# The first norm of a two-layer encoder: row scales as a diagonal in the transposes, the weight behind them, constants loaded later

## The chip, the core and the metric

The kernel runs on one core of a Trainium2 chip. The metric is the device time of one execution in microseconds (us). TensorE (PE) multiplies matrices, and loads their stationary operands (PEld) beside that; VectorE (DVE) and ScalarE (ACT) do elementwise work, GpSimd (POOL) a few small operations. DMAs are issued from SyncE's queue (SP) and from ACT's.

## The reference

One sequence of 256 tokens, width 1024, runs through two layers of: a SwiGLU, four mixers side by side, a second SwiGLU, each between two RMS norms. All is float32. What the change touches is the very first norm and the start of the first SwiGLU:

```python
def rms_norm(x, g):
    y = xf * lax.rsqrt(jnp.mean(xf * xf, axis=-1, keepdims=True) + RMS_EPS)
    return (y * g).astype(x.dtype)

def swiglu(h, w_gate, w_up, w_down):
    return (silu(h @ w_gate) * (h @ w_up)) @ w_down
...
    h = rms_norm(x, g[0])
    x = x + 0.5 * rms_norm(swiglu(h, w_gate, w_up, w_down), g[1])
```

## The kernel before

The 256 tokens are two row tiles (tk 0 and 1) of 128. Products keep float32 precision by splitting both operands into a rounded part and a remainder, hi and lo, and adding three products (`TERMS`): hi*hi, hi*lo, lo*hi. Weights come from HBM in chunks of 128x1024 (512 KB, `f_raw`, four buffers), one DMA each on SP's queue (`Stream.next`, L243); ACT makes `f_hi` and DVE `f_lo`. The first four chunks are split in halves of 512 columns (`SPLITC`). A chunk's DMA waits until the DVE remainder of the chunk four places ahead has released the buffer.

The norm is `norm_t` (L284 and on), for one row tile: ACT squares the two halves of x and sums (`jk`), DVE adds the sums (`st`), POOL takes the power -0.5 (`r_n`), DVE multiplies x by the norm's weight (`xg`, with `gain`, the weight broadcast to all 128 rows: 512 KB), DVE and ACT scale half of `xg` each by the row scale (L297 and the line behind). Then `turn` transposes `xg` in eight 128x128 pieces on TensorE (`pt`, L310) into two PSUM tiles of four pieces, and ACT and DVE split them into the hi and lo of `XT`, 256 columns at a time (L315). `XT` holds the transposed, normed input: `XT_00` to `XT_03` have two of the eight pieces k each, for both row tiles.

The first SwiGLU starts before all is there. `half_block(0, 0)` (`pgh`, L395) multiplies row tile 0 with the first block's gate and up weights (chunks f0 for k 0 to 3 and f1 for k 4 to 7) as soon as its norm is done; then the second norm's `turn` runs, then row tile 1 of the same block (`half_block(0, 1)`). From block 1 on (`block`: `pg`, L418 and L419, chunks f2 and f3; then f4 and f5) both row tiles go together. `rows` (L438) is the down product `y`, with a chunk of its own for each block: f6 is the first. In the program names end in a number; in the order of the kernel before, f0, f1, f2 and f3 are `f_raw_144`, `152`, `222` and `230`, f4 to f6 are `238`, `244` and `250`, and their split parts have slightly higher numbers.

Instructions are written in the order of the functions, and a scheduling layer then places them in each engine's queue and adds the semaphores; eight semaphores serve the DMAs in turn, so that a DMA also waits for one some places ahead. `WARM` products of zeros keep TensorE busy before x arrives. `load_small(l)` loads the constants `C`, the decay logits `lg` and the parameters `par`; `held` places its instructions behind those in `mid`, which are ACT's and DVE's last of an early block of the first SwiGLU; with no DMA among them, the DMAs of `load_small(0)` stand near the start of SP's queue.

Of the kernel before, what the change touches and what calls it, by code (L numbers as in the profile page):

```python
# [9 lines left out]
F32 = mybir.dt.float32  # L10
F32R = mybir.dt.float32r
BF16 = mybir.dt.bfloat16
# [5 lines left out]
P = 128  # L18
# [87 lines left out]
def tile_encoder(ctx: ExitStack, tc: tile.TileContext, x_in, wffn, win, wout, gains, params, idn, cst, rel, out, dbg=None):  # L106
# [31 lines left out]
    def stt(out, a, s, b, op0, op1):  # L138
        V.scalar_tensor_tensor(out=out, in0=a, scalar=s, in1=b, op0=op0, op1=op1)  # L139

    def act(out, a, f, **kw):
        return A.activation(out, a, f, **kw)  # L142
# [4 lines left out]
    def f(a):  # L147
        return a.bitcast(F32)
# [13 lines left out]
    def s1(name, shape=(P, S), dt=F32):  # L162
        return sp.tile(list(shape), dt, tag="s1", bufs=4, name=name)
# [63 lines left out]
    @contextmanager  # L227
    def held(*ins):

        with ExitStack() as c:  # L230
            for i in ins:
                c.enter_context(tc.issue_after(i.ins))
            yield

    class Stream:
# [4 lines left out]

        def next(self, pool=None):
            r = rawp.tile([P, 1024], F32, tag="raw", name=f"{self.name}raw{self.i}")
            nc.sync.dma_start(out=r, in_=self.dram[:, self.i * 1024:(self.i + 1) * 1024])  # L243
            if self.first and self.i == 1:
                load_x(1, 0)
                load_x(1, 1)
            new = pool or (w4, w4)
            hi = new[0]([P, 1024], F32R, name=f"{self.name}hi{self.i}")
            lo = new[1]([P, 1024], F32R, name=f"{self.name}lo{self.i}")
            n = 2 if self.i < SPLITC else 1  # L250
            with held(*self.hold.get(self.i, ())):
                for c in range(n):
                    cs = slice(c * 1024 // n, (c + 1) * 1024 // n)
                    act(hi[:, cs], r[:, cs], AF.Copy)
                    sub(lo[:, cs], r[:, cs], f(hi[:, cs]))
            self.i += 1
            return hi, lo
# [3 lines left out]
    def gain(l, i):  # L261
        t = k4([P, D], name=f"gain{l}_{i}")
        nc.scalar.dma_start(out=t, in_=gains[l, i:i + 1, :].broadcast_to([P, D]))
        return t

    def rstd(ms, n, name):
        r = sp.tile([P, 8], F32, tag="rstd", bufs=4, name=name)
        tt(r[:, 0:n], ms, nhalf[:, 0:n], ALU.pow, G)
        return r
# [9 lines left out]
    def xt2(XT, k):  # L279

        return XT[k // 2][:, k % 2, :, :]

    def norm_t(XT, g, tk, tag, hold=()):

# [70 lines left out]


    TA, TB, TC, SG = 4, 2, 5, 2
    NPRO, NEPI, SPLITC, WARM, W_FIN, ZW = 3, 7, 4, 8, 4.0, 2
    RATIO, RATIO2, W_PREP, W_INV, GRAIN, R1, R2, WQ, QG, KD = 0.8, 0.6, 4, 12, 0.8, 1.4, 2.2, 0.12, 8, 2

    def ffn(hold, l, j, XT, before2, ahead, after, first, last, mix_next):
# [126 lines left out]
        for fb in range(fb0, NFB - 3):  # L488
            fetch_ab(fb + 1)
            fetch_d(fb + 1)  # L490
            early = block(fb + 1)
            if fb == fb0 + 3:
                mid = early
            rows([fb], 0)
            if fb < NFB - NEPI:
                rows([fb], 1)
# [808 lines left out]
    gi = {("f", 0): 0, ("m", 0): 2, ("f", 1): 4}  # L1305
    XT = new_xt(0, 0)
    load_x(0, 0)
    g0 = gain(0, 0)
    load_x(0, 1)
    nc.sync.dma_start(out=ident, in_=idn)  # L1310
    act(warm, ones1, AF.Silu)

    pq = ps.tile([P, 256], F32, tag="o", bufs=1, name="pq")
    z = SB[0][0].rearrange("p a b c -> p (a b c)")
    for i in range(WARM):
        T.matmul(pq, lhsT=z[:, 0:P], rhs=z, start=True, stop=True)
    done = norm_t(XT, g0, 0, "d")()
    pend = lambda: norm_t(XT0, g0, 1, "a", done[1])
    XT0, done = XT, {0: done[0], 1: done[1]}
    for n, (kind, l, j) in enumerate(seq):  # L1320
        i = gi[(kind, j)]
# [118 lines left out]
```

## Time and profile before

| | |
|---|---|
| time, median of 3 runs | 1170.97 us (1168.13 to 1174.04) |
| profiled execution | 1175.67 us, of which the span of instructions 1174.0 us |
| granted TensorE clock, mean | 0.984 |
| busy: PE / PEld / DVE / ACT / POOL | 97 / 82 / 68 / 55 / 8% of the span |
| read from HBM | 187.62 MB, 161 GB/s over the span |

The page gives busy times of each engine over the whole span; the part that the change touches is its first 26 us, for which the timeline (each instruction's start and length, and in brackets the idle time before it and what ended it) and the waits are read. L121, L139 and L142 are helpers that issue most elementwise work of DVE and ACT, so those instructions are told apart by their tiles.

### The profile page before, as it was taken

To read this page: it belongs to the slowest core of one execution; us is meant where nothing else is said; L and a number is where in the kernel's file an instruction comes from. 1 tells how busy PE (TensorE), PEld (TensorE's weight loads), DVE (VectorE), ACT (ScalarE), POOL (GpSimd) and SP (SyncE) were. 2 spreads that over 40 slices of the span, in tenths; PEclk is the share of its full clock that TensorE was granted. 3 is DMA by queue.
4 is the path that set the end of the run, shared out by engine and by line. 5 is a ranking of instruction groups with operands and counts; after the bars stand their busy time and mean duration, and the time that the engine had idled before them with its cause. 6 is when DMAs were issued, how large, how long until landed. Compare 5 with 4: busy or idle time off the path is not lost. (4 is left out here: it accounts for less than half of the span.)

```text
span 1174.0 us, 20406 instructions
## 1 busy us (share of the span) xinstructions
PE 1133.7 (97%) x8084; PEld 966.0 (82%) x8084; DVE 799.9 (68%) x1351; ACT 641.9 (55%) x1159; POOL 92.3 (8%) x159
## 2 busy tenths in 40 slices
PE   7999999979999999999999999999799999999997
PEld 6888888877888888887788888889778888888886
DVE  6656566797775866665676666667896669565663
ACT  6565555757333655554655555557473357455562
POOL 0000000243100000000000000013431000000000
PEclk9999999987999999999999999999899999999999
DMA  7755574412341665656546656725124326565650
GB/s 276 238 181 189 188 237 140 156 33 82 101 133 58 220 215 182 195 181 211 186 128 210 197 180 196 231 94 180 50 72 145 110 82 207 196 189 188 190 187 36
DMA packets 53088, 189.99 MB, mean 162 GB/s; under 512 B 6144, under 2 KB 6272, under 8 KB 52992
## 3 DMA queue, kind: packets, MB, share of 16 engines
q1 hardware_dynamic: 50976, 181.61, 47.6%
q10 hardware_dynamic: 2016, 7.08, 1.7%
q8 instruction: 63, 1.03, 0.4%
q14 instruction: 33, 0.27, 0.1%
HBM read 187.62 MB, written 1.05 MB: 161 GB/s over the span
## 5 line engine op out<-in xcount | busy, mean ns | idle before, releaser
L121 DVE TENSOR_TENSOR f_lo<-f_raw,f_hi 128x1024 fp32r<-128x1024 f32 (+1 forms) x280 | 323.7, 1162 | 201.1 <-ACT f_hi L142 200.2
L418 PE MATMUL pg<-XT,f_hi 128*128 128x512 f32 x1248 | 444.4, 398 | 3.5 <-DVE gu L121 3.4
L142 ACT ACTIVATE f_hi<-f_raw 128x1024 fp32r<-128x1024 f32 (+1 forms) x280 | 280.1, 1008 | 138.2 <-DMA f_raw<-in_wffn_dram 95.1
L419 PE MATMUL pg<-XT,f_lo 128*128 128x256 f32 x1248 | 350.0, 280 | 0.0
L418 PEld LDWEIGHTS pg<-XT,f_hi 128*128 128x128 f32 x1248 | 234.4, 188 | 62.7 <-DVE gu L121 6.4
L419 PEld LDWEIGHTS pg<-XT,f_lo 128*128 128x128 f32 x1248 | 235.6, 189 | 2.7
L438 PE MATMUL y<-f_hi,hT 128*128 128x512 f32 x704 | 233.5, 393 | 2.2 <-ACT hT L142 1.2
L438 PEld LDWEIGHTS y<-f_hi,hT 128*128 128x128 f32 x704 | 131.6, 188 | 33.7 <-DVE hT L121 2.7
L351 PE MATMUL pz<-XT,i_hi 128*128 128x256 f32 x704 | 146.9, 303 | 1.2 <-ACT zp L142 1.2
L438 PE MATMUL y<-f_lo,hT 128*128 128x512 f32 x352 | 138.0, 392 | 0.3 <-DVE f_lo L121 0.3
L351 PEld LDWEIGHTS pz<-XT,i_hi 128*128 128x128 f32 x704 | 114.3, 197 | 13.8 <-issue 7.0
L351 PE MATMUL pz<-XT,i_lo 128*128 128x256 f32 x352 | 103.1, 293 | 0.9 <-DVE i_lo L121 0.9
L142 ACT ACTIVATE hT<-gu 128x256 fp32r<-128x256 f32 x78 | 32.6, 418 | 126.3 <-DVE gu L121 126.3
L121 DVE TENSOR_TENSOR i_lo<-i_raw,i_hi 128x1024 fp32r<-128x1024 f32 (+1 forms) x68 | 75.6, 1127 | 19.5 <-ACT i_hi L142 18.6
L142 ACT ACTIVATE i_hi<-i_raw 128x1024 fp32r<-128x1024 f32 (+1 forms) x68 | 63.8, 953 | 41.5 <-PE pz L351 17.0
L121 DVE TENSOR_TENSOR gu<-pg,gu 128x256 f32<-128x256 f32 x156 | 65.2, 418 | 15.2 <-ACT gu L142 15.2
L438 PEld LDWEIGHTS y<-f_lo,hT 128*128 128x128 f32 x352 | 66.1, 188 | 11.5 <-DVE f_lo L121 0.8
L351 PEld LDWEIGHTS pz<-XT,i_lo 128*128 128x128 f32 x352 | 69.6, 198 | 2.7 <-DVE i_lo L121 1.5
L142 ACT ACTIVATE gu<-pg 128x256 f32<-128x256 f32 x156 | 57.6, 369 | 19.2 <-PE pg L419 18.6
L121 POOL TENSOR_TENSOR r_y<-st,nhalf 128x1 f32<-128x1 f32 x12 | 6.5, 540 | 772.5 <-DVE st L139 772.5
L395 PE MATMUL pgh<-f_hi,XT 128*128 128x256 f32 x320 | 61.8, 287 | 2.3 <-DVE XT L315 2.3
L431 DVE TENSOR_TENSOR hT<-gu,hT 128x256 fp32r<-128x256 f32 x78 | 33.1, 425 | 34.9 <-ACT hT L142 34.9
(292 smaller groups left out, 1359.0 us busy)
## 6 DMA issues: line engine op xcount, KB each, us to landing
f_raw<-in_wffn_dram SPq DMA_DIRECT2D x264, 512.0 KB, 4.2
i_raw<-in_win_dram SPq DMA_DIRECT2D x60, 512.0 KB, 3.7
o_raw<-in_wout_dram SPq DMA_DIRECT2D x16, 512.0 KB, 3.7
gain<-in_gains_dram ACTq DMA_DIRECT2D x12, 512.0 KB, 5.3
x<-in_x_dram SPq DMA_DIRECT2D x4, 256.0 KB, 6.7
out_dram<-x SPq DMA_DIRECT2D x4, 256.0 KB, 2.0
rl<-in_rel_dram ACTq DMA_DIRECT2D x2, 384.0 KB, 6.0
C<-in_cst_dram SPq DMA_DIRECT2D x1, 573.0 KB, 7.8
```

Source lines behind the costliest of these rows:

```text
L121: eng.tensor_tensor(out=out, in0=a, in1=b, op=op)
L142: return A.activation(out, a, f, **kw)
L351: T.matmul(dst, lhsT=w[a][:, k * P:(k + 1) * P], rhs=xt(XT, k, b), start=n == 0, stop=n == 23)
L395: T.matmul(pg, lhsT=xt(XT, k, a)[:, tk * P:(tk + 1) * P], rhs=w[b][:, c:c + 256], start=n == 0, stop=n == 23)
L418: T.matmul(pg, lhsT=w[0][:, c:c + P], rhs=xt2(XT, k), start=k == 0, stop=False, skip_group_check=True)
L419: T.matmul(pg[:, 0, :], lhsT=w[1][:, c:c + P], rhs=xt(XT, k, 0), start=False, stop=k == 7, skip_group_check=True)
L431: V.tensor_tensor(out=hT[:, 1, :], in0=h, in1=f(hT[:, 0, :]), op=ALU.subtract))
L438: ins = T.matmul(y[tk][h], lhsT=hts[fb][:, a, tk * P:(tk + 1) * P], rhs=ws[fb][2][b][:, h * 512:(h + 1) * 512], start=fb == 0 and i == 0, ...
```

## The change

`norm_first` replaces `norm_t` for the first norm alone, for both row tiles. DVE multiplies the identity by the row scales (`dg`, 128x128), and TensorE multiplies each piece of x, as it came from HBM, with this diagonal: that transposes and scales in one. They are products of full float32 and no longer transposes by the identity. The norm's weight is loaded as 8x128 (`g8`, 4 KB), turned by one small transpose into `gT` (128x8), and applied as a scale for each partition when ACT and DVE split the pieces, 128 columns at a time. The pieces alternate between the two PSUM tiles. The identity and `g8` are loaded on ACT's queue, x has the first places in SP's; the first two weight chunks come in two DMAs each. Two warm-up products are left out. `mid` now also has the DMA of the last chunk issued there, so that the loads in `load_small(0)` follow it.

```diff
         def next(self, pool=None):
-            nc.sync.dma_start(out=r, in_=self.dram[:, self.i * 1024:(self.i + 1) * 1024])
+            n = 2 if self.first and self.i < 2 else 1
+            for c in range(n):
+                o = self.i * 1024
+                self.dma = nc.sync.dma_start(out=r[:, c * 1024 // n:(c + 1) * 1024 // n],
+                                             in_=self.dram[:, o + c * 1024 // n:o + (c + 1) * 1024 // n])
...
+    def norm_first(XT, gT, tk, tag, hold=()):
+        st = sp.tile([P, 3], F32, tag="st", bufs=4, name="st")
+        for h in range(2):
+            jk = sp.tile([P, 512], BF16, tag="jk", bufs=1, name="jk")
+            with held(*hold):
+                act(jk, x[tk][h], AF.Square, scale=1.0 / 32.0, accum_out=st[:, h:h + 1])
+        stt(st[:, 2:3], st[:, 0:1], RMS_EPS, st[:, 1:2], ALU.add, ALU.add)
+        r = rstd(st[:, 2:3], 1, "r_n")
+        dg = s1("dg", (P, P))
+        scaled = V.tensor_scalar(out=dg, in0=ident, scalar1=r[:, 0:1], scalar2=None, op0=ALU.mult)
+
+        def turn():
+            pts = [ps.tile([P, 4, P], F32, tag=tag, bufs={"a": PA, "y": PY}[tag], name="pt") for i in range(2)]
+            for k in range(8):
+                T.matmul(pts[k % 2][:, k // 2, :], lhsT=x[tk][k // 4][:, (k % 4) * P:(k % 4 + 1) * P], rhs=dg,
+                         start=k < 2, stop=True, skip_group_check=True)
+            for k in range(8):
+                hi, lo = (XT[k // 2][:, k % 2, a, tk * P:(tk + 1) * P] for a in range(2))
+                src, gk = pts[k % 2][:, k // 2, :], gT[:, k:k + 1]
+                ends[:] = (act(hi, src, AF.Copy, scale=gk),
+                           V.scalar_tensor_tensor(out=lo, in0=src, scalar=gk, in1=f(hi), op0=ALU.mult, op1=ALU.subtract))
+            return (scaled,), ends
...
-    NPRO, NEPI, SPLITC, WARM, W_FIN, ZW = 3, 7, 4, 8, 4.0, 2
+    NPRO, NEPI, SPLITC, WARM, W_FIN, ZW = 3, 7, 4, 6, 4.0, 2
...
-                mid = early
+                mid = early + (st.dma,)
...
     load_x(0, 0)
-    g0 = gain(0, 0)
     load_x(0, 1)
-    nc.sync.dma_start(out=ident, in_=idn)
+    g8 = sp.tile([8, P], F32, tag="par", bufs=1, name="g8")
+    nc.scalar.dma_start(out=ident, in_=idn)
+    nc.scalar.dma_start(out=g8, in_=gains[0, 0].rearrange("(k d) -> k d", d=P))
...
-    pq = ps.tile([P, 256], F32, tag="o", bufs=1, name="pq")
+    pq = ps.tile([P, 256], F32, tag="d", bufs=PD, name="pq")
+    gT = kp.tile([P, 8], F32, name="gT")
     for i in range(WARM):
+        if i == WARM - 2:
+            pgT = ps.tile([P, 8], F32, tag="o", bufs=1, name="pgT")
+            T.transpose(pgT, g8, ident[0:8, 0:8])
+            act(gT, pgT, AF.Copy)
         T.matmul(pq, lhsT=z[:, 0:P], rhs=z, start=True, stop=True)
-    done = norm_t(XT, g0, 0, "d")()
-    pend = lambda: norm_t(XT0, g0, 1, "a", done[1])
+    done = norm_first(XT, gT, 0, "y")()
+    pend = lambda: norm_first(XT0, gT, 1, "a", done[1])
```

The scheduling layer orders the start anew; behind about the 90th instruction of TensorE, the 40th of ACT and the 54th of DVE all engines but SP have the same instructions in the same order as before, and SP only the constants elsewhere. ACT's queue from the last half of chunk f2 to f3, with the second norm's splits between, stands so before (f3 is `f_raw_230`):

```order
L142 ACTIVATE f_hi_224<-f_raw_222 128x512
L142 ACTIVATE hh<-pgh 128x128
L142 ACTIVATE xg<-xg,r_n 128x512
L142 ACTIVATE XT_00_94<-pt 128x2x128
L142 ACTIVATE XT_02_96<-pt 128x2x128
L142 ACTIVATE hT<-ph 128x128
L142 ACTIVATE XT_01_95<-pt 128x2x128
L142 ACTIVATE XT_03_97<-pt 128x2x128
L142 ACTIVATE f_hi_232<-f_raw_230 128x512 x2
```

And now (f2 is `f_raw_236`, f3 `244`, f4 `252`, f5 `258`, f6, the first down chunk, `264`):

```order
L142 ACTIVATE hh<-pgh 128x128
L142 ACTIVATE f_hi_238<-f_raw_236 128x512
L142 ACTIVATE hT<-ph 128x128
L142 ACTIVATE XT_00_94<-pt,gT 128x128 x2
L142 ACTIVATE XT_01_95<-pt,gT 128x128 x2
L142 ACTIVATE XT_02_96<-pt,gT 128x128 x2
L142 ACTIVATE f_hi_266<-f_raw_264 128x1024
L142 ACTIVATE XT_03_97<-pt,gT 128x128 x2
L142 ACTIVATE f_hi_246<-f_raw_244 128x512 x2
```

The split of the first down chunk stands ahead of the last two splits of the second norm, where it had its place behind f5 before. On DVE the second norm stands so before:

```order
L139 SCALAR_TENSOR_TENSOR st<-st 128x1
L297 TENSOR_SCALAR xg<-xg,r_n 128x512
L121 TENSOR_TENSOR hh<-hh,pgh 128x128
L121 TENSOR_TENSOR f_lo_225<-f_raw_222,f_hi_224 128x512
L315 TENSOR_TENSOR XT_00_94<-pt,XT_00_94 128x2x128
```

and now, up to the remainder of the first down chunk:

```order
L121 TENSOR_TENSOR hh<-hh,pgh 128x128
L298 TENSOR_SCALAR dg<-ident,r_n 128x128
L121 TENSOR_TENSOR f_lo_239<-f_raw_236,f_hi_238 128x512
L121 TENSOR_TENSOR hT<-ph,hT 128x128
L310 SCALAR_TENSOR_TENSOR XT_00_94<-pt,gT,XT_00_94 128x128 x2
L310 SCALAR_TENSOR_TENSOR XT_01_95<-pt,gT,XT_01_95 128x128 x2
L310 SCALAR_TENSOR_TENSOR XT_02_96<-pt,gT,XT_02_96 128x128 x2
L310 SCALAR_TENSOR_TENSOR XT_03_97<-pt,gT,XT_03_97 128x128 x2
L121 TENSOR_TENSOR f_lo_247<-f_raw_244,f_hi_246 128x512 x2
L121 TENSOR_TENSOR f_lo_255<-f_raw_252,f_hi_254 128x1024
L121 TENSOR_TENSOR f_lo_261<-f_raw_258,f_hi_260 128x1024
L121 TENSOR_TENSOR f_lo_267<-f_raw_264,f_hi_266 128x1024
```

DVE still has the remainders of f3, f4, f5 and f6 behind the last split, in that order. TensorE's order at the first down product of the first block (`y`) is now:

```order
L452 MATMUL pg<-XT_03_97,f_lo_247 128x256
L471 MATMUL y_01_283<-f_hi_266,hT 128x512
L471 MATMUL y_00_282<-f_lo_267,hT 128x512
L471 MATMUL y_00_282<-f_hi_266,hT 128x512
L451 MATMUL pg<-XT_00_94,f_hi_238 128x512
```

As before, the product with the remainder of f6 stands ahead of the second half of block 1, so TensorE's queue waits there for that remainder.

More of the change, by code (lines that the diff above doesn't have):

```diff
@@ L281, in xt2 @@
         return XT[k // 2][:, k % 2, :, :]
+    def norm_first(XT, gT, tk, tag, hold=()):
[19 more added lines that the diff above has]
+            return (scaled,), ends
+        ends = []
+        return turn
     def norm_t(XT, g, tk, tag, hold=()):
```

## The prediction

> **What bounds the kernel now.** I read the page's busy times first, then the stretches of the first 186 us, then what TensorE waits for, then the timeline of the start.
>
> ```profile
> span 1174.0 us, 20406 instructions
> PE 1133.7 (97%) x8084; PEld 966.0 (82%) x8084; DVE 799.9 (68%) x1351; ACT 641.9 (55%) x1159; POOL 92.3 (8%) x159
> ...
> 9.40:12.20 2.80, 1.09 (x8) 0.86 (x8) 2.01 (x6) 2.31 (x6) 0.00 (x0) 1.00 1.05 418
> 12.20:17.20 5.00, 3.39 (x24) 2.99 (x24) 4.30 (x10) 4.37 (x11) 0.55 (x1) 1.00 0.94 349
> 17.20:25.40 8.20, 7.82 (x51) 6.60 (x51) 7.49 (x13) 6.35 (x14) 0.00 (x0) 1.00 0.69 197
> 25.40:186.00 160.60, 159.56 (x842) 135.92 (x843) 103.09 (x150) 91.97 (x149) 0.00 (x0) 1.00 0.63 210
> ```
>
> The last four rows give, for a stretch, its length and the busy time of PE, PEld, DVE, ACT and POOL, then clock, DMA share and GB/s. From 25.4 to 186 us TensorE is busy 159.56 of 160.60 us. So whatever the change does before 25.4 us is carried to the end unshortened, and nothing that it does to other engines later counts unless it makes TensorE wait. The question is only: when does TensorE come to the work that it does at 25.4 us now? From 9.4 to 25.4 us DVE and ACT are also nearly full, and they hand TensorE its operands.
>
> ```profile
> 5.78 0.63 ACT L142 ACTIVATE jk<-x 128x512 bf16<-128x512 f32 x1 [3.04 <-DMA x<-in_x_dram]
> 6.57 1.33 DVE L121 TENSOR_TENSOR xg<-x,gain 128x512 f32<-128x512 f32 x2 [4.56 <-DMA gain<-in_gains_dram]
> 7.28 0.63 ACT L142 ACTIVATE jk<-x 128x512 bf16<-128x512 f32 x1 [0.77 <-DMA x<-in_x_dram]
> 8.34 0.54 POOL L121 TENSOR_TENSOR r_n<-st,nhalf 128x1 f32<-128x1 f32 x1 [7.20 <-DVE st L139]
> 8.91 0.49 DVE L297 TENSOR_SCALAR xg<-xg,r_n 128x512 f32<-128x512 f32 x1 [0.72 <-POOL r_n L121]
> 9.46 1.09 PE L310 MATMUL pt<-ident,xg 128*128 128x128 f32 x8 [1.51 <-DVE xg L297]
> 12.21 0.39 PE L395 MATMUL pgh<-f_hi,XT 128*128 128x256 f32 x1 [1.65 <-DVE XT L315]
> ...
> 12.80 1.14 ACT L142 ACTIVATE f_hi<-f_raw 128x512 fp32r<-128x512 f32 x2
> 13.46 1.29 DVE L121 TENSOR_TENSOR f_lo<-f_raw,f_hi 128x512 fp32r<-128x512 f32 x2
> 15.59 0.62 ACT L142 ACTIVATE f_hi<-f_raw 128x512 fp32r<-128x512 f32 x1
> ```
>
> These are the first norm and the first half-block: start, length, instruction, and in brackets the wait. The second half of x is there at 7.28; 1.63 us later its scale is applied, and at 9.46 the transposes start. The gain (6.57) is not the last to come: the second half of x is.
>
> ```profile
> 17.23 1.09 PE L310 MATMUL pt<-ident,xg 128*128 128x128 f32 x8 [1.45 <-DVE xg L297]
> 18.34 0.86 DVE L315 TENSOR_TENSOR XT<-pt,XT 128x256 fp32r<-128x256 f32 x2 [0.37 <-ACT XT L142]
> 19.59 0.76 DVE L315 TENSOR_TENSOR XT<-pt,XT 128x256 fp32r<-128x256 f32 x2
> 20.39 1.29 DVE L121 TENSOR_TENSOR f_lo<-f_raw,f_hi 128x512 fp32r<-128x512 f32 x2
> 21.85 3.50 DVE L121 TENSOR_TENSOR f_lo<-f_raw,f_hi 128x1024 fp32r<-128x1024 f32 x3 [0.17 <-ACT f_hi L142]
> 25.40 0.50 PE L438 MATMUL y<-f_lo,hT 128*128 128x512 f32 x1 [0.32 <-DVE f_lo L121]
> ```
>
> This is the second norm and the last wait before TensorE is full: the product y<-f_lo with the first down chunk needs DVE's fifth remainder after the second norm's last split (20.35). DVE does them without a break, 20.39 to 25.35, and TensorE takes the product at 25.40. This is the end point on which the sum is made.
>
> **The change, part by part.** Prices first:
>
> ```profile
> L142 ACT ACTIVATE hT<-ph 128x128 fp32r<-128x128 f32 x2 | 0.5, 274 | 0.3 <-PE ph L405 0.3
> L142 ACT ACTIVATE xg<-xg,r_n 128x512 f32<-128x512 f32 x4 | 2.9, 724 | 3.3 <-POOL r_n L121 3.3
> L142 ACT ACTIVATE f_hi<-f_raw 128x512 fp32r<-128x512 f32 x8 | 4.8, 626 | 0.0
> L121 DVE TENSOR_TENSOR hT<-ph,hT 128x128 fp32r<-128x128 f32 x2 | 0.6, 286 | 0.1
> L431 DVE TENSOR_TENSOR hT<-gu,hT 128x256 fp32r<-128x256 f32 x21 | 8.9, 424 | 8.2 <-ACT hT L142 8.2
> L139 DVE SCALAR_TENSOR_TENSOR zs<-sh,dv,zs 128x256 f32<-128x256 f32 x8 | 3.8, 480 | 2.2 <-POOL sh L121 1.9
> 1.25 6.70 PE L1316 MATMUL pq<-SB 128*128 128x256 f32 x16 [1.25 <-DVE SB L197]
> f_raw<-in_wffn_dram SPq DMA_DIRECT2D x1, 512.0 KB, 3.7
> par<-in_params_dram SPq DMA_DIRECT2D x1, 279.0 KB, 4.0
> C<-in_cst_dram SPq DMA_DIRECT2D x1, 573.0 KB, 7.8
> 0.80 0.85 SPq L176 DMA_DIRECT2D x<-in_x_dram  x2
> 21.71 35.63 SPq L243 DMA_DIRECT2D f_raw<-in_wffn_dram  x18
> 75.17 0.19 ACT L142 ACTIVATE pair<-C 128x8 fp32r<-128x8 f32 x1
> ```
>
> The first six rows are groups: count, busy time, mean ns of one, idle time before. The DMA rows give the time from issue to landing, in us.
>
> *Earlier x.* The 512 KB gain no longer shares the DMA engines with the first 512 KB of x. The two halves are issued 0.4 us apart (0.85 for two), the second at 1.2. A lone 279 KB transfer took 4.0 us, so it lands near 5.3; bounds are 4.7 (a little faster than that row) and 7.28 (no earlier than now). Its square then follows the other half's, at about 5.6. The two further issues that the split of the first weight chunks adds to SP, about 0.4 us each, stand in front of the second x rows only; those wait for the identity's landing and come long before their use at 13.4. ident and the 4 KB weights, two issues on ACT's queue, lie ahead of its table load and are hidden by the wait for x. Six warm-up products (6.70/8 each) and one small transpose end near 6.6, before the norm needs TensorE.
>
> *The scale as a diagonal.* From square to scaled diagonal takes the 1.63 us of now plus a 128-wide scaling, 0.2 us (bounds 0.16 and the 0.49 of the 512-wide one): the first product starts at 7.45 instead of 9.46, **2.0 us earlier**. No DVE product with the gain and no scaling of xg remains, 1.36 us of DVE and 0.72 of ACT for each row tile.
>
> *The transposes become fp32 products,* two passes each. Eight one-pass transposes take 1.09 us; less the tail of the last, 0.27, they follow each other by 0.117. Sixteen passes so cost 1.9 us; the upper end is the warm-up's pass, 6.70/16 = 0.42 for 256 columns, 0.21 for 128, or 3.4 us. I take 1.9, by the row with the same tile width: **0.8 us more**, twice. As the order stands, ACT's first split waits for the seventh product (one bank holds every second chunk), so nearly all of it is exposed.
>
> A page speaks against the change here. The granted clock column reads 1.00 from the start, yet the warm-up passes cost 0.42 us. The Trainium skill, "TensorE: Matmul & The Clock Gate", Part 1, says that the array runs at half rate until a free-running window of about 3.4 us has been busy. By it the products could still meet the half rate, at 7.45 us, where the transposes at 9.46 did not; the rows support that the start is slow, and do not show when it ends. It is rival B.
>
> *The weight applied in the split.* Eight pieces of 128 columns replace four of 256. A piece on ACT costs 0.274 and, for a scale read from memory, 0.10 more (0.724 against 0.626): 0.375. On DVE 0.286 plus the 0.06 by which the three-operand form is dearer (0.480 against 0.424): 0.345. With two banks, ACT's next piece of a bank waits for DVE's piece of it, so a pair costs 0.375 + 0.345 + two hand-overs of 0.04 = 0.8, four pairs 3.2 us. Bounds: 0.64 without the surcharges (2.6), and 1.0 if bank reads cost DVE more (4.0). First row tile: splits 9.35 to 12.75. TensorE's first half-block starts at 9.7 instead of 12.21, **2.5 us earlier**, but its second half needs the second weight chunk, which ACT splits after all eight pieces: from 12.3 instead of 12.80, its remainder done at 14.25 instead of 14.75. Only **0.5 us** of the gain is left there.
>
> *The second norm* starts from that point. ACT's row of squares and splits, 12.80 to 16.2 now, comes 0.5 us earlier; the diagonal is ready and products start at 16.5 instead of 17.23 (0.7 earlier). The products take 0.8 more: splits start at 18.35 instead of 17.92. They need 3.2 us, and **between the third and the fourth pair ACT now has the split of the first down chunk**, 1.06 us. That chunk's DMA can only start when DVE has released the raw buffer of the third chunk, at 17.1 as the second half of its remainder follows the diagonal; it takes 3.7 and lands at 20.8, when ACT is free at 20.6. So 0.2 + 1.06 us stand in the splits: the last ends at 18.35 + 3.2 + 1.26 = 22.8 instead of 20.35. Behind that DVE has the same five remainders, 5.0 us and 0.2 for the wait on ACT: the down product runs at 28.0 instead of 25.40, **2.6 us later**. TensorE has work until about 24.9 and then waits 3 us.
>
> *Constants later.* C, lg and par go from the start to behind the 22nd weight chunk, about 51 us (18 chunks, the eighth to the 25th, are issued from 21.71 over 35.63 us); pair reads C at 75.2, and C, the largest, takes 7.8 us now. Their four issues (1.7 us) and 0.85 MB lie on a queue that waits for buffers anyway while TensorE does not. Hidden, at nothing; were that cover gone, the lag of 0.85 MB at the 418 GB/s of the second stretch would be 2 us. Taking them from the start shortens no wait above, since the chunks there wait for buffers, not for bytes. POOL keeps its two powers, and the PSUM tags move no wait.
>
> Sum: -2.0 at the first product, +0.8 for it, +0.8 for the second, +3.0 for slower splits and the chunk among them: +2.6 at the end point. The profiled run took 1175.67 us for its 1174.0 us span, 4.7 us above the median of three, 1170.97. Its new time is 1178.3; on the median's footing **1173.6 us**.
>
> **Rivals.**
>
> A, it ends faster. If ACT and DVE do not alternate by bank but run side by side, a pair costs about 0.4: each of the two split stages is 1.6 us shorter and the end point comes at 24.8, 0.6 us early: 1170.4. For it speaks that there are two banks; against it, that the waits in the order chain them. It decides below a pair of about 0.5 us.
>
> B, the norm products meet the slow array: 0.21 us a pass for the first eight, 1.5 us more, everything behind it as late: 1175.1. If both norms' products cost that much, for a reason of fp32 and not of the clock, the second 1.5 us adds: 1176.6. Against both speaks the row of 1.09 us.
>
> C, the new 3 us wait of TensorE lowers its clock. The trace has one such case:
>
> ```profile
> 256.40:260.00 3.60, 0.00 (x0) 0.51 0.00 0
> 260.00:270.10 10.10, 9.64 (x44) 0.50 0.46 141
> ...
> 260.03 1.65 PE L757 MATMUL pgr<-ar,bk 64*128 64x128 f32 x6 [5.61 <-ACT GR L142]
> ```
>
> After a wait of 5.61 us the granted clock was 0.50 until 270. Waits of 1.5 to 1.7 us did not do it. If 3 us does, half of the ten us that follow are lost, 5 us: 1178.6, slower by 0.65%. The same section of the Trainium skill's page on TensorE has the clock fall after an idle window of about 3.4 us, which a wait of 3 us cannot hold; the trace has nothing between 1.7 and 5.6 us to test it.
>
> D, x lands no earlier than now, with everything 1.7 us later than in my sum: 1175.3.
>
> **How the numbers follow.** My forecast has 0.58, A 0.15, B 0.14, C 0.06, D 0.07. Runs of the kernel before scatter by 3 us either way, so A's low end is about 1168.5 and B's second case or C reach 1178.5: the range 1168.5 to 1178.5 holds 8 in 10 or a little more. The likeliest case alone, with the bounds of the split and the scatter, is 1170.5 to 1177. About 0.5%, 5.9 us, is what a measurement of this kernel can tell from no change: slower by more is C and the tail of B, 0.10; faster by more would need 6 us from a start in which TensorE's quoted waits (1.51, 1.65, 1.45 and 0.32) sum to 4.9, 0.03; the rest is 0.87.
>
> **What would show it.** Right: the first norm product near 7.5, the first half-block near 9.7, ACT's split of the down chunk between the second norm's third and fourth pair, and the product y<-f_lo near 28 with TensorE waiting about 3 us for it. Wrong: a pair of splits well under 0.8 us, passes of 0.2 us, a granted clock of 0.5 after 25 us, or TensorE waiting for a chunk after 30 us, which would mean that the moved constants collide.

## The result and the profile after

| | kernel before | changed kernel |
|---|---|---|
| time, median of 7 runs each | 1171.06 us (1168.13 to 1175.92) | 1178.21 us (1175.96 to 1184.54) |
| ratio of the times | 1 | 1.0063, 95% interval 1.0039 to 1.0088 |
| profiled execution, its span | 1175.67 us, 1174.0 us | 1178.15 us, 1176.4 us |
| product y<-f_lo with the first down chunk (the end point) | 25.40 us | 28.95 us |

The change makes the kernel slower: by 7.15 us in the medians, 4.6 to 10.3 us by the interval. The time lies within the predicted range; the likeliest case, 2.6 us later, was too low, and the loss is just beyond the half per cent that the prediction took as measurable. The profiled runs differ by only 2.4 us of span, because the profiled run of the kernel before was 4.6 us above its median.

The page's span and busy times of the changed kernel:

```profile
span 1176.4 us, 20449 instructions
...
PE 1138.2 (97%) x8097; PEld 969.8 (82%) x8097; DVE 798.7 (68%) x1355; ACT 641.4 (55%) x1166; POOL 92.3 (8%) x159
```

TensorE is busy 4.5 us longer, with its weight loads 3.8; VectorE, ScalarE and GpSimd are within 1.2 us of before. So TensorE's own work is looked at first. The timeline of the changed kernel's start follows, engine by engine (start, length, instruction, and in brackets the idle time before it with what ended it). L304 are the products of x and the diagonal dg, L310 DVE's half of the splits, L428 the half-blocks, L471 the down product.

```profile
4.67 0.63 ACT L142 ACTIVATE jk<-x 128x512 bf16<-128x512 f32 x1
8.74 0.62 ACT L142 ACTIVATE XT<-pt,gT 128x128 fp32r<-128x128 f32 x2 [0.65 <-PE pt L304]
9.52 0.63 ACT L142 ACTIVATE XT<-pt,gT 128x128 fp32r<-128x128 f32 x2 [0.16 <-DVE XT L310]
...
19.55 2.37 ACT L142 ACTIVATE XT<-pt,gT 128x128 fp32r<-128x128 f32 x6 [2.80 <-PE pt L304]
21.81 1.05 ACT L142 ACTIVATE f_hi<-f_raw 128x1024 fp32r<-128x1024 f32 x1
22.76 0.62 ACT L142 ACTIVATE XT<-pt,gT 128x128 fp32r<-128x128 f32 x2
```

```profile
12.28 1.29 DVE L121 TENSOR_TENSOR f_lo<-f_raw,f_hi 128x512 fp32r<-128x512 f32 x2 [0.17 <-ACT f_hi L142]
...
23.15 0.61 DVE L310 SCALAR_TENSOR_TENSOR XT<-pt,gT,XT 128x128 fp32r<-128x128 f32 x2 [0.85 <-ACT XT L142]
23.93 1.29 DVE L121 TENSOR_TENSOR f_lo<-f_raw,f_hi 128x512 fp32r<-128x512 f32 x2 [0.17 <-ACT f_hi L142]
25.40 3.50 DVE L121 TENSOR_TENSOR f_lo<-f_raw,f_hi 128x1024 fp32r<-128x1024 f32 x3 [0.17 <-ACT f_hi L142]
```

```profile
6.92 1.95 PE L304 MATMUL pt<-dg,x 128*128 128x128 f32 x16
9.16 0.39 PE L428 MATMUL pgh<-f_hi,XT 128*128 128x256 f32 x1 [0.29 <-ACT XT L142]
...
12.30 0.39 PE L428 MATMUL pgh<-f_hi,XT 128*128 128x256 f32 x1 [1.23 <-ACT f_hi L142]
...
16.23 3.71 PE L304 MATMUL pt<-dg,x 128*128 128x128 f32 x16
...
28.95 0.50 PE L471 MATMUL y<-f_lo,hT 128*128 128x512 f32 x1 [2.38 <-DVE f_lo L121]
```

The order is the one foreseen: the first norm ends early, TensorE then waits 1.23 us for the second weight chunk, ACT's split of the first down chunk stands between the third and the fourth pair of the second norm, and TensorE waits 2.38 us for the down chunk's remainder. But the second norm's sixteen passes took 3.71 us where the first norm's took 1.95. The stretches of 3.4 us say why (length, then the busy time of PE, PEld, DVE, ACT and POOL, then the granted clock):

```profile
10.20:13.62 3.42, 1.85 (x13) 1.42 (x12) 2.85 (x8) 3.14 (x9) 0.00 (x0) 1.00 0.73 298
13.62:17.03 3.41, 2.72 (x14) 2.41 (x13) 2.15 (x6) 1.96 (x6) 0.55 (x1) 0.50 0.47 154
17.03:20.45 3.42, 3.39 (x16) 3.10 (x16) 0.47 (x3) 0.84 (x3) 0.00 (x0) 0.50 0.50 153
20.45:24.00 3.55, 3.55 (x28) 3.37 (x28) 2.36 (x8) 3.43 (x9) 0.00 (x0) 1.00 0.02 5
```

From 13.62 to 20.45 us the granted clock was 0.50. The profiled run of the kernel before has no such stretch between 7.3 us and the end point. Whether it belongs to the change or to the run was the first question for the experiments.

### The profile page after: what moved, and what is told of

Read it like the earlier page. It is cut to its first block, busy times and chain, and to the rows that moved or that the text cites. A ratio compares the mean times of both kernels' runs of the same rounds, so it can differ in the third digit from the quotient of the medians.

```text
span 1176.4 us, 20449 instructions
## 1 busy us (share of the span) xinstructions
PE 1138.2 (97%) x8097; PEld 969.8 (82%) x8097; DVE 798.7 (68%) x1355; ACT 641.4 (55%) x1166; POOL 92.3 (8%) x159
## 5 line engine op out<-in xcount | busy, mean ns | idle before, releaser
L471 PE MATMUL y<-f_hi,hT 128*128 128x512 f32 x704 | 234.6, 395 | 1.2 <-ACT hT L142 0.6
L471 PEld LDWEIGHTS y<-f_hi,hT 128*128 128x128 f32 x704 | 131.6, 188 | 32.2 <-DVE hT L121 2.3
L471 PE MATMUL y<-f_lo,hT 128*128 128x512 f32 x352 | 137.7, 391 | 2.4 <-DVE f_lo L121 2.4
L471 PEld LDWEIGHTS y<-f_lo,hT 128*128 128x128 f32 x352 | 66.2, 188 | 14.5 <-DVE f_lo L121 2.7
L428 PE MATMUL pgh<-f_hi,XT 128*128 128x256 f32 x320 | 62.8, 290 | 2.2 <-ACT f_hi L142 1.2
```

The costliest lines, as they stand in the source:

```text
L428: T.matmul(pg, lhsT=xt(XT, k, a)[:, tk * P:(tk + 1) * P], rhs=w[b][:, c:c + 256], start=n == 0, stop=n == 23)
L471: ins = T.matmul(y[tk][h], lhsT=hts[fb][:, a, tk * P:(tk + 1) * P], rhs=ws[fb][2][b][:, h * 512:(h + 1) * 512], start=fb == 0 and i == 0, ...
```

## Experiments

Two theories. T, dataflow: the loss is the longer norm products, the paired splits and the down chunk, as far as they move the end point. U, clock: the loss is mostly that the change makes TensorE run at half rate more often. Later, when the time had turned out larger than the end point, P (the products) stood against K (the moved constants) and S (the splits). Every kernel was timed in five rounds beside the kernel before on its own chip; each ratio is to that. The end point is read in the one profiled run of each kernel, the half-rate stretch from its clock column; the slow warm-up at the very start, which that column does not show, is left out.

| kernel | ratio to before, 95% interval | end point, us | half rate before 35 us | behind at the same clock, us |
|---|---|---|---|---|
| changed, first runs | 1.0063 (1.0039 to 1.0088) | 28.95 | 13.6 to 20.4 | |
| changed, once more | 1.0051 (1.0024 to 1.0078) | 26.77 | none | 6.4 |
| constants early | 1.0047 (1.0018 to 1.0075) | 27.08 | none | 5.3 |
| down chunk behind the splits | 1.0054 (1.0020 to 1.0088) | 26.70 | none | 5.0 |
| products of zeros in the gap | 1.0030 (1.0004 to 1.0055) | 27.23 | 27.8 to 31.2 | 3.6 |
| norm products twice | 1.0083 (1.0051 to 1.0115) | 32.73 | 15.4 to 22.2, 32.4 to 35.8 | 7.1 |
| one-pass transposes of a scaled x | 1.0014 (0.9987 to 1.0041) | 27.29 | 13.1 to 20.0 | 0.6 |
| the same, and the down chunk behind | 1.0018 (0.9990 to 1.0045) | 26.05 | none | 2.1 |
| the same, and the zeros | 1.0031 (1.0002 to 1.0060) | 25.85 | 26.8 to 30.2 | 3.1 |
| before, fp32 products alone | 1.0031 (1.0006 to 1.0057) | 28.55 | 9.7 to 13.2 | 6.0 |
| before, constants later alone | 1.0037 (1.0004 to 1.0070) | 27.07 | 11.5 to 18.4 | 2.0 |
| before, data part with constants | 1.0001 (0.9977 to 1.0026) | 27.38 | 11.8 to 18.6 | 0.2 |
| before, data part without them | 0.9999 (0.9973 to 1.0025) | 26.52 | 10.2 to 17.0 | -0.5 |

The last column is an estimate, worked out from the 258 runs behind the other rows: a straight line of the time on the run's mean granted clock, with an offset for each chip and each kernel. The time falls by 0.90 us for each 0.001 of clock, and the runs scatter by 2.2 us about that line (standard deviation) instead of 4.0. Each figure is uncertain by 1.4 to 1.6 us (95%). What a kernel pays through a lower clock is not in it.

### The changed kernel once more

No edit. 

> The changed kernel once more, on a second chip beside the other variants. Theory T, dataflow: its cost is what the end point shows without a half-rate stretch in the start, 2.4 us, with one 3.5 us: ratio 1.002 to 1.003, so the first comparison (1.0063) was high by chance of the runs' scatter. Theory U, clock: the change lowers the clock in more runs than the kernel before has it: ratio 1.005 to 1.007 again, with a mean granted clock 0.002 to 0.003 below that of the kernel before. The trace tells whether the stretch from 13.6 to 20.4 us is at half rate again: T says it comes and goes with the phase of the windows, since a variant with the same gap had none.

```profile
6.60 2.05 PE L304 MATMUL pt<-dg,x 128*128 128x128 f32 x16 [0.23 <-DVE dg L298]
...
15.49 2.05 PE L304 MATMUL pt<-dg,x 128*128 128x128 f32 x16
...
26.77 0.50 PE L471 MATMUL y<-f_lo,hT 128*128 128x512 f32 x1 [2.43 <-DVE f_lo L121]
```

In this run's start (PE rows of its timeline) both norms' passes are at full rate and the end point is 1.37 us later than before, not 3.55. So the half-rate stretch belongs to the run: T was right on that. But the ratio was 1.0051, which T had at 1.002 to 1.003, and U's explanation fails too: the mean granted clock of its runs was 0.9852, that of the kernel before beside it 0.9847 (the first seven runs had 0.9813). The kernel is slower at the same clock, by 6.4 us (4.9 to 7.9), and that is more than this start shows.

### The down chunk behind the second norm's splits

```
-                    st.hold.update({3: r[1], 4: r[1]})
+                    st.hold.update({3: r[1], 4: r[1], 6: r[1]})
```

> The changed kernel, with the split of the first down chunk held behind the last split of the second norm (before it stood between the third and the fourth pair, 1.05 us at 21.81). Theory T, dataflow (the loss is the longer products, the paired splits and this chunk): the last split ends about 1.1 us earlier, at 22.7, the five remainders follow, and y<-f_lo starts near 27.8 instead of 28.95; the time falls by about 1.1 us, 1178.2 to 1177.1, so some 6 us behind the kernel before (ratio 1.005). Theory U, clock (most of the loss is TensorE at half rate in more stretches than before): the same at the end point, but the granted clock stays where it was (about 0.982) and the products of the second norm still take 3.7 us. Rival: the down chunk is then late itself, its remainder waits, and the end point doesn't move.

ACT and DVE rows of its timeline:

```profile
19.74 0.63 ACT L142 ACTIVATE XT<-pt,gT 128x128 fp32r<-128x128 f32 x2 [0.16 <-DVE XT L310]
20.27 3.98 ACT L142 ACTIVATE f_hi<-f_raw 128x512 fp32r<-128x512 f32 x5
...
22.40 1.23 DVE L121 TENSOR_TENSOR f_lo<-f_raw,f_hi 128x1024 fp32r<-128x1024 f32 x1 [0.18 <-ACT f_hi L142]
24.28 2.36 DVE L121 TENSOR_TENSOR f_lo<-f_raw,f_hi 128x1024 fp32r<-128x1024 f32 x2 [0.66 <-ACT f_hi L142]
```

The rival won. The fourth pair now follows the third at once, DVE's last split ends at 20.75 instead of 21.59 in the repeat, and the end point is 26.70 instead of 26.77. What the splits gained, DVE lost in two waits for ACT, 0.18 and 0.66 us, because ACT had the same five chunks still to do, 3.98 us without a break, and DVE's second whole chunk waited for the last of them (until 24.25). As the queues are ordered, the chunk among the splits costs nothing.

### Products of zeros in the gap

```
...
+                if k == 4 and first and fb == 0 and tk == 0:
+                    busy(3, ins)        # three 128x256 fp32 products of zeros, behind the last product of k = 3
```

> The changed kernel, with three fp32 products of zeros (six passes of 256 columns, results not used) put into TensorE's queue behind the first half of the first half-block, where it waited 1.23 us for the second weight chunk (11.07 to 12.30). Theory U: that gap is what brought the half rate from 13.62 to 20.45; with the gap filled the stretch stays at full rate, the second norm's sixteen passes take 1.95 us instead of 3.71, and the end point comes 1.0 to 1.8 us earlier (1.0 if ACT then waits for the down chunk's DMA). Theory T: the stretch is run to run scatter that the gap doesn't set; the passes take 1.95 or 3.71 us as in a run of the changed kernel, the dummies cost 0 to 0.2 us, and the time stays at 1178.

```profile
11.18 1.46 PE L423 MATMUL pb<-SB 128*128 128x256 f32 x6
...
15.98 2.05 PE L304 MATMUL pt<-dg,x 128*128 128x128 f32 x16
```

```profile
24.40:27.82 3.42, 1.03 (x6) 0.62 (x5) 3.31 (x5) 1.41 (x3) 0.00 (x0) 1.00 0.87 226
27.82:31.23 3.41, 3.41 (x12) 2.92 (x11) 1.26 (x2) 1.65 (x3) 0.00 (x0) 0.50 0.98 353
```

The first fence has PE rows of the timeline, the second two stretches of the same run. No half rate at 13.6, but the repeat had none there either, without the zeros, so this run decides nothing about the gap. Instead the wait of 2.39 us for y<-f_lo brought a half-rate stretch, 27.82 to 31.23. The end point is 0.46 us later than in the repeat because TensorE came out of its slow warm-up later: the norm products start at 7.03 us instead of 6.60. The ratio, 1.0030, is lower than that of the other kernels with these products, within the intervals.

### The products undone

```
-        dg = s1("dg", (P, P))
-        scaled = V.tensor_scalar(out=dg, in0=ident, scalar1=r[:, 0:1], scalar2=None, op0=ALU.mult)
+        xg = k4([P, D], name="xg")
+        scaled = V.tensor_scalar(out=xg[:, 0:512], in0=x[tk][0], scalar1=r[:, 0:1], scalar2=None, op0=ALU.mult)
+        scaled2 = act(xg[:, 512:1024], x[tk][1], AF.Copy, scale=r[:, 0:1])
...
-                T.matmul(pts[k % 2][:, k // 2, :], lhsT=x[tk][k // 4][:, (k % 4) * P:(k % 4 + 1) * P], rhs=dg,
-                         start=k < 2, stop=True, skip_group_check=True)
+                T.transpose(pts[k % 2][:, k // 2, :], xg[:, k * P:(k + 1) * P], ident)
```

> The changed kernel, with the products of x and the scaled diagonal undone: DVE scales the first half of x and ACT the second (512 columns each) and the transposes are the one-pass ones of before, with the weights still applied in eight splits of 128. T: scaling takes 0.5 to 0.7 us instead of 0.29, the eight passes 1.1 us instead of sixteen 1.95, so each norm is 0.4 to 0.6 us shorter; the second, when the passes are at half rate, saves up to 1.7: end point 0.8 to 2.2 us earlier, time 1176 to 1177.4. U: the time stays at 1178 with a clock of 0.982, since the passes are not where the loss is.

The same with the down chunk behind, and with the zeros as well:

> The changed kernel with one-pass transposes of a scaled x in place of the products with the diagonal, and with the split of the first down chunk held behind the second norm's last split. T: both gains add: end point 27.3 less 1.1, near 26.2, or 25.2 when no half-rate stretch falls in the start (25.4 in the kernel before); ratio 1.000 to 1.001. U: 1.003 or more, as for the hold alone (1.005), with the end point near 26: then time is lost behind the end point, in waits or half-rate stretches after 30 us.

> The same as the variant with both, and three fp32 products of zeros (results not used) in TensorE's 1.2 us gap of the first half-block. T: end point 25.0 to 25.6 with no half-rate stretch before 25 us; ratio 0.999 to 1.001: the best of the variants on the changed kernel, and not measurably better than the kernel before. U: as the variant with zeros alone, 1.003, because the rows behind the end point lose time that the start doesn't show.

PE rows of the first of the three, then of the second:

```profile
6.89 1.10 PE L305 MATMUL pt<-ident,xg 128*128 128x128 f32 x8
...
16.17 1.97 PE L305 MATMUL pt<-ident,xg 128*128 128x128 f32 x8
...
27.29 0.50 PE L471 MATMUL y<-f_lo,hT 128*128 128x512 f32 x1 [1.78 <-DVE f_lo L121]
```

```profile
7.01 1.09 PE L305 MATMUL pt<-ident,xg 128*128 128x128 f32 x8 [1.05 <-DVE xg L298]
...
15.71 1.09 PE L305 MATMUL pt<-ident,xg 128*128 128x128 f32 x8 [0.29 <-DVE xg L298]
...
26.05 0.51 PE L471 MATMUL y<-f_lo,hT 128*128 128x512 f32 x1 [2.33 <-DVE f_lo L121]
```

A one-pass norm takes 1.1 us at full rate and 1.97 at half, against 1.95 to 2.05 and 3.71 for the products. The ratios fall to 1.0014 and 1.0018, not measurably slower than before, where the kernels with the products beside them on the same two chips had 1.0054 and 1.0051: 4.7 and 3.9 us, each uncertain by about as much. At the same clock the two differences are 4.4 and 4.3 us, each uncertain by 1.8, so undoing the products does help there. T's end point came out in the first. In the second it was 26.05 where T had 25.2 without half rate, in the third 25.85 where T had 25.0 to 25.6. The third then met half rate behind the wait for y<-f_lo (26.8 to 30.2), and its ratio, 1.0031, is the one that U had named. It is no lower than the 1.0030 of the products beside the same zeros, a difference of 0.4 us at the same clock, uncertain by 2.0; so this third pair shows no gain, and why is open. None of the three beats the kernel before.

### The products doubled

```
-            for k in range(8):
+            for k in list(range(8)) * 2:
                 T.matmul(pts[k % 2][:, k // 2, :], lhsT=x[tk][k // 4][:, (k % 4) * P:(k % 4 + 1) * P], rhs=dg,
```

> The changed kernel with both norms' eight fp32 products made twice (the second round overwrites the first): the suspected cost doubled. Sixteen more passes at 0.12 us are 1.9 us more ahead of each norm's splits. P: the first norm's 1.9 us is partly taken up where ACT and DVE wait anyway, the second's is not: end point 2.5 to 3.9 us later than with the changed kernel, 29.3 to 30.7 at full rate, and the time later by the same: ratio 1.007 to 1.009. If the time grows by far more than the end point (ratio over 1.010), a delay in the start is made longer further down. K: the same at the end point; ratio as P has it, since both carry the delay unshortened. If the ratio stays at 1.005, the end point doesn't set the time.

```profile
6.67 3.84 PE L304 MATMUL pt<-dg,x 128*128 128x128 f32 x32 [0.38 <-DVE dg L298]
...
17.79 5.89 PE L304 MATMUL pt<-dg,x 128*128 128x128 f32 x32
...
32.73 0.80 PE L471 MATMUL y<-f_lo,hT 128*128 128x512 f32 x1 [2.25 <-DVE f_lo L121]
```

The end point came 5.65 us later than in the variant with early constants on the same chip (32.73 against 27.08), 2 us beyond the forecast because more than half of the second norm's passes ran at half rate. The ratio, 1.0083, was within it: 0.0036 more, 4.2 us for 32 further passes, uncertain by some 3. In the two profiles the delay stays as it is: the products behind TensorE's two longest waits, pgr<-ar,bk, come 5.93 us later near 265 us (268.81 against 262.88) and 5.87 us later near 845 (848.32 against 842.45). A delay in the start is carried on; it is not multiplied further down.

### The products alone, in the kernel before

```
-                T.transpose(pt[:, k, :], xg[:, (q * 4 + k) * P:(q * 4 + k + 1) * P], ident)
+                T.matmul(pt[:, k, :], lhsT=xg[:, (q * 4 + k) * P:(q * 4 + k + 1) * P], rhs=ident, start=k == 0, stop=True,
+                         skip_group_check=True)
```

This in the first norm's two row tiles only. 

> The kernel before with one part of the change alone, brought to the least: the sixteen transposes of both norms are fp32 products with the identity (two passes each) in place of one-pass transposes; gain, scale, splits of 256, queues and constants are those of before. Theory P: the change's loss comes from the products more than from the splits; twice eight passes more cost 0.9 us each at full rate and 1.8 at half, of which the first bank's splits hide 0.4, since a bank of this layout is full after four chunks: end point 26.4 to 28.5, ratio 1.001 to 1.003. Rival S, splits: the loss is in the paired splits of 128 that only the changed norm has; then the products alone cost under 0.5 us: end point below 26, ratio within 0.999 to 1.001.

```profile
9.42 3.52 PE L311 MATMUL pt<-ident,xg 128*128 128x128 f32 x16 [1.96 <-DVE xg L297]
...
18.56 2.05 PE L311 MATMUL pt<-ident,xg 128*128 128x128 f32 x16 [1.46 <-DVE xg L297]
...
28.55 0.73 PE L442 MATMUL y<-f_lo,hT 128*128 128x512 f32 x2 [1.33 <-DVE f_lo L121]
```

Ratio 1.0031 (1.0006 to 1.0057): the products alone make the kernel before slower by 3.6 us, 0.7 to 6.7; at the same clock by 6.0, 4.4 to 7.6. End point and ratio lie just above P's ranges. S had the end point below 26, so it falls there; the ratio's interval just reaches S's, the estimate at the same clock does not. The end point has a half-rate stretch in it that other variants with one-pass transposes have as well, so its 28.55 is not the price of the products alone.

### The constants and the data part

Constants back to the start in the changed kernel; later in the kernel before:

```
-                mid = early + (st.dma,)      # changed kernel
+                mid = early
...
-                mid = early                  # kernel before
+                mid = early + (st.dma,)
```

> The changed kernel with its constants (C, lg, par) where the kernel before has them, among the first ten weight chunks. What is open: the changed kernel is 0.5 to 0.6% slower, and its start accounts for 1.4 us (full rate) to 3.5 us (half rate from 13.6 to 20.4) of some 6.5. Theory P, products: the two norms' products and splits are all of it, wherever the constants stand: ratio to the kernel before 1.004 to 1.006 again. Theory K, constants: moving them costs about 4 us in the weight stream (the kernel before with the constants alone moved came to 1.0037, with an interval from 1.0004): ratio 1.001 to 1.003, and end point 26.8 or a little later.

> The kernel before with the constants (C, lg, par) behind the 22nd weight chunk and nothing else. T: hidden, ratio 0.999 to 1.001, end point 25.4 as before. Rival: the 0.85 MB collides with weight chunks near 53 us, or takes the order of later work another way, and costs 2 us: ratio 1.002 or more with a wait of TensorE between 50 and 100 us.

The data part (x first, gain behind it, identity on ACT's queue, first two chunks in two DMAs; the edit for the chunks is that of the change and is not shown) in the kernel before, with the constants later and without:

```
     load_x(0, 0)
-    g0 = gain(0, 0)
     load_x(0, 1)
-    nc.sync.dma_start(out=ident, in_=idn)
+    nc.scalar.dma_start(out=ident, in_=idn)
+    g0 = k4([P, D], name="gain0_0")
+    nc.sync.dma_start(out=g0, in_=gains[0, 0:1, :].broadcast_to([P, D]))
```

> The kernel before, with the data part of the change alone: both halves of x first in SP's queue, the gain behind them, the identity on ACT's queue, the first two weight chunks in two DMAs each, the constants later. The norm is the one of before (gain and scale on x, one-pass transposes, four splits of 256). T: x is there by 4.7, the gain near 7.0; xg's products end at 8.3 and the transposes start near 8.9 instead of 9.46; the end point is 0 to 0.6 us earlier, the time 1170.5 to 1171 (ratio 0.999 to 1.000). So the loss would lie in the norm part wholly. U: if moved transfers and constants lower the granted clock later, the ratio is 1.003 or more with the norm of before.

> The kernel before with x first in its queue, the gain behind it, the identity on ACT's queue and the first two chunks in two DMAs each, the constants where they were: the data part without the constants. K: the variant with the constants moved came to 1.0001, so without that move it gains about 4 us: ratio 0.997, faster than both kernels. P: the gain behind x lands at 8.3 as in that variant, its products still end the wait, and the transposes start near 9.6: ratio 0.999 to 1.001, no measurable change.

Moving the constants back gave 1.0047 against 1.0051, as P had it, and the data part without the move, which K put at 0.997, came to 0.9999: K isn't borne out. The kernel before with the constants alone moved had 1.0037 where T had 0.999 to 1.001; the interval almost touches 1. The rival's ratio came, but not its mechanism: TensorE waits for nothing between 45 and 100 us. With the whole data part the ratio was 1.0001, as T had it, while T's early end point was not (27.38, with half rate, and transposes at 9.61 instead of 8.9). In the trace with the constants alone moved ACT's chunk order also changed: DVE's second whole chunk waits 0.67 us for the third that ACT splits (until 24.63):

```profile
24.65 2.36 DVE L121 TENSOR_TENSOR f_lo<-f_raw,f_hi 128x1024 fp32r<-128x1024 f32 x2 [0.67 <-ACT f_hi L142]
...
27.07 0.50 PE L438 MATMUL y<-f_lo,hT 128*128 128x512 f32 x1 [1.16 <-DVE f_lo L121]
```

At the same clock the move costs 2.0 us in the kernel before (0.5 to 3.4), 1.1 in the changed kernel and 0.7 beside the data part (each uncertain by 2). So K's 4 us are excluded, and a cost of 1 to 2 us is likelier than none. The data part gains nothing with the norm of before, because the gain, now behind x, ends the wait in x's place (DVE row, last kernel of the table):

```profile
8.36 1.29 DVE L121 TENSOR_TENSOR xg<-x,gain 128x512 f32<-128x512 f32 x2 [2.84 <-DMA gain<-in_gains_dram]
```

x first pays only for a norm that needs no broadcast weight, and that norm gave the gain back.

## Why the prediction was right or wrong

Its steps, against the first profile (half rate from 13.6) and the repeat (full rate), in us:

| step | predicted | first profile | repeat |
|---|---|---|---|
| square of x's second half | 5.6 | 4.67 | 4.62 |
| first norm product | 7.45 | 6.92 | 6.60 |
| its sixteen passes | 1.9 | 1.95 | 2.05 |
| a pair of splits | 0.8 | 0.79 | 0.79 |
| first half-block | 9.7 | 9.16 | 8.94 |
| remainder of f1 done | 14.25 | 13.57 | 13.36 |
| second norm's products | 16.5 | 16.23 | 15.49 |
| their sixteen passes | 1.9 | 3.71 | 2.05 |
| f6's split, wait for its DMA | 20.8, 0.2 | 21.81, none | 19.63, none |
| last split done | 22.8 | 23.76 | 21.59 |
| y<-f_lo | 28.0 | 28.95 | 26.77 |

*Right.* The direction and its reason: an early first norm whose gain is nearly lost at the second weight chunk, and a second norm with longer products and splits. The pair of 0.8 us (ACT's 0.63 for two pieces, then 0.16 of waiting for DVE) is measured as worked out, so rival A falls. The constants at no cost are nearly right: 4 us are excluded, 1 to 2 us are not.

*Too cautious.* x's second half was squared from 4.62 on, not 5.6: the first product came 0.85 us earlier than said in the repeat, and rival D falls. With the missing DMA wait this is most of why the repeat's end point is 1.37 us later and not 2.6.

*Luck.* The time, 1178.21, lies 0.3 us inside the upper end of the range. That end was set by rival B's second case and by rival C, and neither profile of the changed kernel shows either of them as priced; the likeliest case ended at 1177. A loss of more than half a per cent had 0.10. Rival B missed the first norm narrowly. The clock column reads 1.00 in the warm-up because the trace's record of the clock only begins at 7.31 us in the kernel before, at 6.80 in the first profile and at 5.34 in the repeat. Until then the passes of 256 columns are 0.43 us apart, behind that 0.22, so the same four warm-up passes took 1.92 us in the first profile and 1.21 in the repeat (PE rows, in that order):

```profile
5.16 1.92 PE L1355 MATMUL pq<-SB 128*128 128x256 f32 x4
```

```profile
5.16 1.21 PE L1355 MATMUL pq<-SB 128*128 128x256 f32 x4
```

In the first profile the norm products started at 6.92, 0.12 us behind the end of the slow start.

*Wrong.* The step that failed is the price of the sixteen passes, 0.8 us for each norm. The row that carried it, one-pass transposes, was at full rate, and at full rate the price holds (1.95 to 2.05 us against 1.09). In other runs one of the two norms meets half rate, and then sixteen passes take 3.5 to 3.7 us and eight one-pass transposes 1.97, 1.6 to 1.7 us more instead of 0.8. Rival B named this price, 0.21 us a pass, for the first norm; in the profiled run it fell on the second. By the runs, the products alone cost 3.6 us (0.7 to 6.7), at the same clock 6.0 (4.4 to 7.6), where the prediction had 1.6; taking them out of the changed kernel saves 4.4 and 4.3 us in two pairs of kernels, and nothing that can be measured in the third, with the zeros. So the term is too small, but by more than the passes themselves take in any profile: how the products cost the rest is not shown.

A second step had the wrong cause. The 1.26 us for the down chunk among the splits is not a cost: the variant without it ended 0.07 us earlier. In that variant ACT has five chunks to split behind the splits, and DVE waits for the last of them at its fourth remainder, so the sum was to be made on ACT's work and its order as well as on DVE's.

Rival C, a lower clock behind the wait for y<-f_lo, does occur, but not in the changed kernel's two profiles, which had waits of 2.38 and 2.43 us: after waits of 2.39, 2.33 and 2.25 us in three variants, for one stretch of 3.4 us, so some 1.7 us of work, not five. The prediction took the clock to fall after 5.61 us of waiting. The trace of the kernel before says otherwise: that wait began at 254.42, and the clock fell at 256.48, after this stretch, in which TensorE was busy for 40%:

```profile
253.06:256.48 3.42, 1.36 (x10) 1.04 (x9) 3.29 (x5) 0.00 (x0) 2.37 (x3) 1.00 0.01 2
```

*Open.* Against the one profile of the kernel before, the start explains 1.4 us (repeat) to 3.5 us (first profile) of the 6 to 7 us that the medians differ by; 3.6 to 4.6 us remain. That profile is a favourable reference: it has no half rate between its warm-up and its end point, while all four variants built on that kernel have some, with end points of 26.5 to 28.6. Since these variants are not all slower, half rate in the start is not particular to the change. The same shows further down, at the first product behind TensorE's longest wait, pgr<-ar,bk. It starts at 260.03 in the kernel before, at 262.2 to 262.5 in the three variants with its norm, and at 262.1 to 263.2 in the changed kernel's two profiles and the variants with early constants and with the down chunk behind. So against the variants the changed kernel is at most 1 us late there, and most of the loss is not in the start.

Where it lies is not shown. The repeat and the one-pass transposes with the chunk behind have the same mean clock, 0.990, and spans of 1175.8 and 1170.8 us. At pgr<-ar,bk they are 0.62 us apart the first time (262.84 and 262.22) and 3.89 the second (PE rows, in that order):

```profile
842.52 1.65 PE L790 MATMUL pgr<-ar,bk 64*128 64x128 f32 x6 [5.62 <-ACT GR L142]
```

```profile
838.63 1.65 PE L790 MATMUL pgr<-ar,bk 64*128 64x128 f32 x6 [5.63 <-ACT GR L142]
```

Part of that is 1.7 us in which TensorE waits for `gu` of DVE between 600 and 800 us in the repeat, and not at all in the other. But such waits come with the norm of before too (1.1 us with the constants later, 1.0 with the data part without them), so they are not particular to the change either. The loss isn't in the mean clock or the down chunk.

## What to carry to other kernels

Where a chain of small steps feeds a full TensorE, an early first step is worth only what the next operand allows; here 3 us at the first half-block shrank to 1.2 to 1.4 at the second weight chunk, whose split waited behind the norm's own. Before a transpose is turned into an fp32 product to save elementwise work, price its passes at full and at half rate, since a start with gaps may meet either. Moving one piece of work out of a chain gains nothing where a second engine still has it to do ahead of what is needed next. One profile of each kernel cannot place a difference of half a per cent. Comparing runs at the same mean clock nearly halves their scatter, and it is worth doing before a cause is named.

## What the runs showed of the hardware

Every half-rate stretch that the clock column shows, but for the one that the end cuts off, lasted one to five times 3.41 us. In the first 35 us, each window of that length in which TensorE was busy 43% of the time or less was followed by half rate; between 51 and 57% it went either way, three windows at 54% falling and ten others not, and above 57% none fell. The windows are counted from the clock's first record, 4.3 to 7.3 us into the run; the slow warm-up ahead of it is not among them. From the kernel before, its data part with the constants, and the products alone:

```profile
7.31:10.72 3.41, 1.73 (x11) 1.05 (x9) 1.77 (x4) 2.50 (x6) 0.54 (x1) 1.00 1.03 401
10.72:14.13 3.41, 1.82 (x13) 1.61 (x13) 3.37 (x9) 2.61 (x7) 0.00 (x0) 1.00 1.04 421
```

```profile
8.38:11.79 3.41, 1.09 (x8) 0.86 (x8) 2.44 (x6) 2.24 (x5) 0.00 (x0) 1.00 1.05 411
11.79:15.20 3.41, 2.66 (x12) 2.66 (x13) 3.38 (x8) 2.80 (x8) 0.00 (x0) 0.50 0.74 252
```

```profile
6.34:9.75 3.41, 1.45 (x8) 0.97 (x7) 2.00 (x4) 2.19 (x6) 0.54 (x1) 1.00 1.03 409
9.75:13.16 3.41, 3.31 (x17) 3.02 (x15) 2.14 (x4) 1.84 (x5) 0.00 (x0) 0.50 1.01 366
```

With 1.09 and 1.45 us of work in the window the next one is at 0.50, with 1.73 at 1.00; 1.85 us, as the changed kernel had from 10.20 to 13.62, was followed by 0.50. In the repeat the same gap of 1.23 us fell across two windows, which were busy 2.00 and 2.29 us, and nothing followed:

```profile
8.75:12.17 3.42, 2.00 (x13) 1.68 (x13) 2.55 (x9) 2.94 (x10) 0.00 (x0) 1.00 1.02 413
12.17:15.58 3.41, 2.29 (x14) 1.70 (x14) 2.68 (x7) 3.06 (x9) 0.55 (x1) 1.00 0.44 118
```

So what counts is how a gap falls into these windows, which differs from run to run. The Trainium skill, "TensorE: Matmul & The Clock Gate", Part 1, has the clock fall after an idle window of about 3.4 us. The length agrees with the 3.41 us here; the idle window does not: the windows above were busy for a third to a half, and the measurement decides. By that section, as the prediction said, a wait of 3 us could not lower the clock; waits of 1.2 to 2.4 us did, in some of the runs.
